# A hybrid decoder trunk on one core: all transposes of its two mixers through the vector engine and DRAM, and 64-row products in alternate halves of the array

## The chip, the cores and the metric

The kernel runs on one core of a Trainium2 chip. The metric is the device time of one launch in microseconds (us). The kernel before takes 1131.28 us, the median of three runs (1131.26 to 1131.33). Engines are named as in the profile: PE (TensorE, matmul), PEld (its weight load), DVE (VectorE), ACT (ScalarE), POOL (GpSimd) and SP (SyncE, which issues nearly all DMAs here).

## The reference

Two layers over a sequence of 256 tokens of width 1024, in float32:

```python
for i in range(DEPTH):                                   # DEPTH = 2
    x = x + 0.5 * swiglu_ffn(rmsnorm(x, ffn1_norm[i]), ffn1_wi[i], ffn1_wo[i])     # width 2816
    z = rmsnorm(x, mix_norm[i]) @ w_in[i]
    mq, mk, mv, mo, mi, mf, sq, sk, sv, ga, gb = jnp.split(z, offsets, axis=-1)
    hA = mlstm_chunkwise(mq, mk, mv, mi + b_igate[i], mf + b_fgate[i])   # 4 heads, qk 64, v 128
    yA = (jax.nn.sigmoid(mo) * rmsnorm(hA, ml_out_norm[i])) @ w_a[i]
    hB = swa_sink_attention(sq, sk, sv, q_norm[i], k_norm[i], sinks[i], rel_bias)
    yB = hB @ w_b[i]                                     # 8 query heads on 2 key heads of 64
    x = x + (jax.nn.sigmoid(ga) * yA + jax.nn.sigmoid(gb) * yB) @ w_out[i]
    x = x + 0.5 * swiglu_ffn(rmsnorm(x, ffn2_norm[i]), ffn2_wi[i], ffn2_wo[i])
    gate = jax.nn.sigmoid(rmsnorm(x, ple_norm[i]) @ w_ple_gate[i])
    x = x + gate * (p[i] @ w_ple[i])
```

`mlstm_chunkwise` is a causal product of q and k, weighted by exp of sums of gates with a running maximum (the gates' sums F, c and M below), times v, divided by a bounded row sum. `swa_sink_attention` normalises q and k per head, adds a position bias, takes the softmax over a window of 128 with a sink per head, and multiplies by v.

## The kernel before, in words

The 256 tokens stand as two tiles t of 128 rows. Every large product takes activations with the contracted width on the partitions: the left operand of a matmul (the one that PE loads as weights) is the transposed activation, the right one the weight matrix from DRAM. For float32 accuracy each operand is split into a high and a low part, and a product is three matmuls (`mm_unit`, L222 to L224: high by low, low by high, high by high).

Weight matrices come in units of up to 1 MB. SP starts their load into one of three `raw` buffers (L190, tile names raw_*), ACT writes the high part (L194, hi_*) and DVE subtracts for the low part (L195, lo_*), each in two halves of 1024 columns, into a ring of four buffers; loads run three units ahead. PE's order is written by hand: the program runs as a stream of units, and after each tile's 12 matmuls of a unit a `tick()` advances every spawned task, a Python generator, to its next `yield`. The constants W_* are numbers of such ticks that a task lets pass before its matmuls or transposes, so that other engines can finish what they need. DVE, ACT, POOL and SP get their orders from a scheduler that follows PE's program.

The FFN's gated hidden tiles h aren't transposed on PE but by `turn_split`: DVE transposes 32x32 blocks (L254, tile inq), SP writes the result to DRAM (L260, scr) and reads it back with the blocks in their places (L265, back), and ACT and DVE split it into high and low (L273, L274).

In the mixer of a layer, PE transposes against an identity. The projections come in the order sq, if (with keys and values of the window attention), mqk, mv, mo, ga0, ga1, gb0, gb1 (tiles z_mix_*). Spawned beside them:
- `swa`, for the queries and keys of the window attention: qk is normalised to qkn (L563, L569) and PE transposes it after W_NORM ticks (tps L579, tpk L582) to qTs and kTs.
- `ep_mqk`: q and k of the mLSTM, transposed on PE (tpq L530), copied to qT and kT (L533, L534).
- `swa_part`: logits (lg, L606), softmax, transposes of its weights L (pt L634) to PT after W_PT ticks, product with v (ov L648) after W_OV, result hb, transposed (tp_hb, L245) after W_HB.
- `ml_gates`: the gates' sums on 4 rows, in the order emt, c, M, lf, F, c, M, emt (L691 to L702); after W_CP ticks PE turns c and emt into columns (cp, L708 and L709), and M goes over DRAM to all rows (Mb).
- `ml_mix` and `ml_out`: st = k by q (L734, L740) times the weights E, then num (L761 and on) and its row sums dd (L767, L768), normalisation, output gate, result ha, transposed after W_HA ticks (tp_ha, L245).

The heads of lg and st have a width of 64, so that each of these matmuls contracts over one half of the array's 128 rows. In `merged`, ya (from w_a) and yb (from w_b) are gated, summed and transposed on PE (tp_mx). The second FFN follows, and beside it the embedding p is transposed on PE (tp_p). Lines of the changed functions that the diff doesn't touch keep their meaning after it.

Of the kernel before, what the change touches and what calls it, by code (L numbers as in the profile page):

```python
# [52 lines left out]
W_NORM = 5  # L53
# [3 lines left out]
W_OV = 2  # L57
# [3 lines left out]
W_HA = 5  # L61
# [3 lines left out]
def trunk_kernel(ctx: ExitStack, tc: tile.TileContext, a: dict, out: bass.AP):  # L65
# [182 lines left out]
    def turn_split(pool, src, nblk, hi, lo, name):  # L248


        n = nblk * P
# [2 lines left out]
        nc.vector.transpose(  # L254
            inq[:, 0:n].rearrange("p (b k s) -> p b k s", b=4, k=nblk),
            src[:, 0:n].rearrange("p (k c b) -> p b k c", c=32, b=4),
        )
# [15 lines left out]
        nc.scalar.copy(hv, bv)  # L273
        nc.vector.tensor_tensor(lv, bv, hv.bitcast(F32), op=ALU.subtract)  # L274

# [194 lines left out]
    def mix_in(pool, i, xn, finish):  # L470
# [21 lines left out]
        qk = pair([P, 10, HD], "qk")  # L492
# [29 lines left out]
        def ep_mqk(t, o, rstd):  # L522
            z = work.tile([P, 512], F32, tag="sg", name=f"mqk{i}_{t}")
            nc.scalar.activation(z, o, AF.Copy, scale=rstd)

            def turn():
                yield
                tp = bank(f"tpq{i}_{t}")
                for b in range(4):
                    nc.tensor.transpose(tp[:, b * P : (b + 1) * P], z[:, b * P : (b + 1) * P], ident)  # L530
                tv = tp.rearrange("p (b s) -> p b s", s=P)
                tok = slice(t * P, (t + 1) * P)
                nc.vector.tensor_copy(qT[:, :, tok], tv[:, 0:2, :])  # L533
                nc.vector.tensor_scalar(kT[:, :, tok], tv[:, 2:4, :], HD**-0.5, None, ALU.mult)  # L534

            spawn(turn())
# [12 lines left out]
        def swa(t):  # L549
# [27 lines left out]
            tp = bank(f"tps{i}_{t}")  # L577
            for j in range(4):
                nc.tensor.transpose(tp[:, j * P : (j + 1) * P], z[:, j * P : (j + 1) * P], ident)  # L579
            nc.scalar.activation(qTs[t], heads(tp, P), AF.Copy, scale=qs)  # L580
            tk = bank(f"tpk{i}_{t}")
            nc.tensor.transpose(tk[:, 0:P], z[:, 4 * P :], ident)  # L582
            nc.scalar.activation(kTs[:, t * P : (t + 1) * P], tk[:, 0:P], AF.Copy, scale=qg[:, 1:2])
            for h0 in range(0, SWQ, 4 * (2 - t)):
                spawn(swa_part(t, h0))

        def swa_part(t, h0):
# [10 lines left out]
            yield  # L598
            L = pool.tile([P, nh, nk], F32, tag="s4", name=f"L{nmp}", bufs=4)
            mx = stat("mx")  # L600
            for j0 in range(0, nh, per):
                g = (h0 + j0) // 4
                rows = slice(HD * g, HD * (g + 1))
                o = heads(bank(f"lg{nmp}_{j0}"), nk)
                for j in range(per):
                    nc.tensor.matmul(  # L606
                        o[:, j, :], qTs[t][rows, (h0 + j0 + j) % 4, :], kTs[rows, 0:nk], start=True, stop=True
                    )
                js = slice(j0, j0 + per)
                nc.vector.tensor_tensor(L[:, js, :], o, bias[:, h0 + j0 : h0 + j0 + per, boff:], op=ALU.add)  # L610
                nc.vector.reduce_max(mx[:, js], L[:, js, :], axis=AX.X)
# [17 lines left out]
            PT = pool.tile([P, t + 1, nh, P], F32, tag="s4", name=f"PT{nmp}", bufs=4)  # L629
            for kt in range(t + 1):  # L630
                for j0 in range(0, nh, 4):
                    tp = bank(f"pt{nmp}_{kt}_{j0}")
                    for j in range(4):
                        nc.tensor.transpose(  # L634
                            tp[:, j * P : (j + 1) * P], L[:, j0 + j, kt * P : (kt + 1) * P], ident
                        )
                    dst = PT[:, kt, j0 : j0 + 4, :]
                    if kt + j0 == 0:
                        nc.scalar.copy(dst, heads(tp, P))
                    else:  # L640
                        nc.vector.tensor_copy(dst, heads(tp, P))
# [3 lines left out]
            for j in range(nh):  # L645
                g = (h0 + j) // 4
                for kt in range(t + 1):
                    nc.tensor.matmul(  # L648
                        ov[:, j * HD : (j + 1) * HD],
                        PT[:, kt, j, :],  # L650
# [11 lines left out]
            hi, lo = abT[t][1]  # L662
            transpose_split(hb, nh * HD // P, hi[:, ks, :], lo[:, ks, :], f"hb{nmp}")
# [53 lines left out]
        def ml_mix():  # L717
# [12 lines left out]
            for par in range(2):  # L730
                rows = slice(HD * par, HD * (par + 1))
                o = bank(f"st0{i}_{par}").rearrange("p (h t s) -> p h t s", t=2, s=P)
                for hh in range(2):
                    nc.tensor.matmul(o[:, hh], kT[rows, hh, 0:P], qT[rows, hh, :], start=True, stop=True)  # L734
# [4 lines left out]
                for hh in range(2):
                    nc.tensor.matmul(o[:, hh], kT[rows, hh, P:S], qT[rows, hh, P:S], start=True, stop=True)  # L740
                for hh in range(2):
                    ev = E2[:, 2 * hh + par, :]
                    nc.vector.tensor_tensor(ev, ev, o[:, hh], op=ALU.mult)
            for t in range(NT):
                yield
                spawn(ml_out(t, E01, E2))

        def ml_out(t, E01, E2):
# [39 lines left out]
            hi, lo = abT[t][0]  # L788
            transpose_split(haf, 4, hi, lo, f"ha{i}_{t}")
# [34 lines left out]
        for n in range(2):  # L824
            oa = [bank(f"ya{i}_{t}_{n}") for t in range(NT)]
            stream(oa, abTs, [f"wa{i}_{n}_0"], 4)
            ob = [bank(f"yb{i}_{t}_{n}") for t in range(NT)]
            stream(ob, abTs, [f"wb{i}_{n}_0"], 4, kbase=4)
# [42 lines left out]
    for i in range(DEPTH):  # L871
# [6 lines left out]
        with tc.tile_pool(name=f"ple{i}", bufs=1, side="right", reuse_waits="tile") as pool:  # L878
            pT = [halves(pool, 2, f"pT{i}_{t}") for t in range(NT)]

            def embed(_):
# [92 lines left out]
```

## Time and profile before

| what | value |
|---|---|
| median of three runs | 1131.28 us (1131.26 to 1131.33) |
| the profiled execution's own time | 1131.24 us |
| its span | 1129.5 us |
| PE busy, share of the span | 1121.0 us, 99% |
| DVE busy | 722.6 us, 64% |
| ACT busy | 585.3 us, 52% |
| POOL busy | 32.7 us, 3% |
| DMA queue of the hardware | 229.99 MB, 61.5% of 16 engines' span |

The span goes from the first to the last instruction of one execution; the time of an execution is a little longer. Busy PE means that a matmul is in flight there. In a group's row the third number behind the bar is the mean duration of one instruction, for a matmul from its start to its end through the pipeline, so that many of them overlap; the pieces of the chain of waits (start, length, engine, tile, line, count) show their pace. An fp32 matmul that isn't split has two passes in the trace.

### The profile page before, as it was taken

What the parts mean: (1) busy time and instruction counts of PE and PEld (TensorE: products, weight loads), DVE (VectorE), ACT (ScalarE), POOL (GpSimd) and SP (SyncE); (2) the same over time, 40 slices, a digit from 0 to 9 for tenths busy, and PEclk for the clock granted to TensorE, in tenths of its full rate; (3) what the DMA queues carried; (4) which work ended last, traced back from release to release, by engine and by line L of the source; (5) the groups of instructions that cost most, each with busy time, mean ns of one, the idle gap of its engine ahead of it and who ended that gap; (6) DMA issues with size and microseconds to landing.
All of it is one profiled execution on the core that took longest, in us unless ns stands there. A gap on an engine that the chain in (4) does not pass through costs nothing.

```text
span 1129.5 us, 13574 instructions
## 1 busy us (share of the span) xinstructions
PE 1121.0 (99%) x5252; PEld 931.7 (82%) x5252; DVE 722.6 (64%) x916; ACT 585.3 (52%) x848; POOL 32.7 (3%) x30
## 2 busy tenths in 40 slices
PE   8999999999999999999999999999999999999998
PEld 7788888888888888888888888888888888888887
DVE  6775745685677566654776666467856766667454
ACT  6444534677645544543664544347865354444352
POOL 1000000100000000000000000001000000000000
PEclk9999999999999999999999999999999999999999
DMA  7897764744464767765557767555545556776641
GB/s 266 277 302 244 237 228 123 231 161 128 171 196 151 258 224 251 248 220 193 179 165 252 257 228 244 189 158 190 169 143 168 185 184 228 254 245 216 228 147 38
DMA packets 130785, 230.86 MB, mean 204 GB/s; under 512 B 12968, under 2 KB 46880, under 8 KB 130720
## 3 DMA queue, kind: packets, MB, share of 16 engines
q1 hardware_dynamic: 130720, 229.99, 61.5%
q8 instruction: 41, 0.67, 0.2%
q14 instruction: 24, 0.20, 0.1%
HBM read 217.37 MB, written 12.60 MB: 204 GB/s over the span
## 4 chain that ended last, share of the span: by engine, by line
PE 97%; DVE 1%; DMA 1%; issue 0%; ACT 0%; SPq 0%
PE h_f L222 14%; PE h_f L223 14%; PE h_f L224 14%; PE acc_f_o L222 7%; PE acc_f_o L224 7%; PE acc_f_o L223 7%; PE z_mix_ga L222 1%; PE z_mix_ga L224 1%; PE z_mix_ga L223 1%; PE z_mix_gb L222 1%; PE acc_wout L222 1%; PE acc_wout L224 1%; PE z_mix_gb L224 1%; PE acc_wout L223 1%; PE z_mix_gb L223 1%; PE acc_pg L224 1%
## 5 line engine op out<-in xcount | busy, mean ns | idle before, releaser
L195 DVE TENSOR_TENSOR lo_f<-raw_f,hi_f 128x1024 fp32r<-128x1024 f32 (+1 forms) x176 | 207.7, 1216 | 100.6 <-ACT hi_f L194 100.2
L194 ACT CAST hi_f<-raw_f 128x1024 fp32r<-128x1024 f32 (+1 forms) x178 | 176.5, 1039 | 163.1 <-PE h_f L224 90.3
L195 DVE TENSOR_TENSOR lo_f_o<-raw_f_o,hi_f_o 128x1024 fp32r<-128x1024 f32 x88 | 103.7, 1220 | 90.0 <-ACT hi_f_o L194 90.0
L194 ACT CAST hi_f_o<-raw_f_o 128x1024 fp32r<-128x1024 f32 x88 | 88.1, 1050 | 113.7 <-PE acc_f_o L224 70.0
L222 PE MATMUL h_f<-lo_f,xT_f_0h 128*128 128x512 f32 x352 | 138.2, 393 | 0.2 <-DVE lo_f L195 0.2
L223 PE MATMUL h_f<-hi_f,xT_f_0l 128*128 128x512 f32 x352 | 137.1, 390 | 1.2 <-DVE xT_f_0l L239 1.2
L222 PE MATMUL h_f<-lo_f,xT_f_1h 128*128 128x512 f32 x352 | 137.2, 390 | 0.5 <-DVE lo_f L195 0.4
L224 PE MATMUL h_f<-hi_f,xT_f_0h 128*128 128x512 f32 x352 | 137.1, 389 | 0.0
L223 PE MATMUL h_f<-hi_f,xT_f_1l 128*128 128x512 f32 x352 | 137.0, 389 | 0.0
L224 PE MATMUL h_f<-hi_f,xT_f_1h 128*128 128x512 f32 x352 | 136.9, 389 | 0.0
L222 PEld LDWEIGHTS h_f<-lo_f,xT_f_0h 128*128 128x128 f32 x352 | 66.1, 188 | 15.0 <-issue 0.6
L222 PEld LDWEIGHTS h_f<-lo_f,xT_f_1h 128*128 128x128 f32 x352 | 66.0, 188 | 15.0 <-DVE lo_f L195 1.4
L223 PEld LDWEIGHTS h_f<-hi_f,xT_f_0l 128*128 128x128 f32 x352 | 66.2, 188 | 14.8 <-DVE xT_f_0l L239 1.6
L224 PEld LDWEIGHTS h_f<-hi_f,xT_f_1h 128*128 128x128 f32 x352 | 66.1, 188 | 13.9
L224 PEld LDWEIGHTS h_f<-hi_f,xT_f_0h 128*128 128x128 f32 x352 | 66.0, 188 | 13.9
L223 PEld LDWEIGHTS h_f<-hi_f,xT_f_1l 128*128 128x128 f32 x352 | 66.0, 188 | 13.6
L222 PE MATMUL acc_f_o<-lo_f_o,hT_f_1h 128*128 128x512 f32 x176 | 68.8, 391 | 0.0
L222 PE MATMUL acc_f_o<-lo_f_o,hT_f_0h 128*128 128x512 f32 x176 | 68.7, 390 | 0.0
L224 PE MATMUL acc_f_o<-hi_f_o,hT_f_1h 128*128 128x512 f32 x176 | 68.5, 389 | 0.0
L224 PE MATMUL acc_f_o<-hi_f_o,hT_f_0h 128*128 128x512 f32 x176 | 68.5, 389 | 0.0
L223 PE MATMUL acc_f_o<-hi_f_o,hT_f_0l 128*128 128x512 f32 x176 | 68.5, 389 | 0.0
L223 PE MATMUL acc_f_o<-hi_f_o,hT_f_1l 128*128 128x512 f32 x176 | 68.5, 389 | 0.0
(359 smaller groups left out, 2045.7 us busy)
## 6 DMA issues: line engine op xcount, KB each, us to landing
raw_f<-in_ffn_wi_dram SPq DMA_DIRECT2D x79, 1024.0 KB, 5.2
raw_f_o<-in_ffn_wo_dram SPq DMA_DIRECT2D x44, 1024.0 KB, 5.0
scr_h_f<-inq_h_f SPq DMA_DIRECT2D x40, 256.0 KB, 3.9
back_h_f<-scr_h_f SPq DMA_DIRECT2D x40, 256.0 KB, 4.7
raw_f<-in_ffn_wi_dram SPq DMA_DIRECT2D x18, 512.0 KB, 4.4
raw_z_ga<-in_w_in_dram SPq DMA_DIRECT2D x8, 1024.0 KB, 5.4
raw_z_gb<-in_w_in_dram SPq DMA_DIRECT2D x8, 1024.0 KB, 5.3
raw_wout<-in_w_out_dram SPq DMA_DIRECT2D x8, 1024.0 KB, 4.9
```

Source lines behind the costliest of these rows:

```text
L194: nc.scalar.copy(hi[:, o:e], raw[:, o:e])
L195: (nc.gpsimd if between and o // step % 2 == 0 else nc.vector).tensor_tensor(lo[:, o:e], raw[:, o:e], hi[:, o:e].bitcast(F32), op=ALU.subtract
L222: nc.tensor.matmul(o, xh, wl[:, k, sl], start=start, stop=False)
L223: nc.tensor.matmul(o, xl, wh[:, k, sl], start=False, stop=False)
L224: nc.tensor.matmul(o, xh, wh[:, k, sl], start=False, stop=stop)
```

## The change

All transposes inside the mixers and that of the embedding take the way that h has. `turn` is `turn_split` without the split, and can write the turned tile in the order "s k" (token outside, block inside), so that the 4 or 5 blocks of one token lie side by side: qkTs is [128, 256 tokens, 5] (4 query blocks and one of keys), qkT [128, 256, 4], and PT has its four heads innermost. The matmuls of lg, st and ov then read columns with a step of 4 or 5 floats. Gains are put on qkTs in place by ACT; k of the mLSTM is scaled in `ep_mqk`. lg and st use two banks, one for each half of the rows, and alternate between the halves. W_NORM goes from 5 to 2, W_OV from 2 to 1, W_HA from 5 to 3; a turn has ticks of its own, one more than before. w_b is loaded and multiplied before w_a. The inq tiles of the mixers and of the embedding share two buffers (tag "xg") with work tiles, ha shares with qk, and lf is kept in ln. Transposes of x, of the merged mx and of the gates cp remain on PE.

```diff
-W_NORM = 5
+W_NORM = 2
 W_CP = 6
 W_MB = 2
 W_PT = 3
-W_OV = 2
+W_OV = 1
 W_HB = 1
-W_HA = 5
+W_HA = 3
...
-            specs.extend(by_cols(a["w_a"][i], 512, cols, f"wa{i}_{n}"))
             specs.extend(by_cols(a["w_b"][i], 512, cols, f"wb{i}_{n}"))
+            specs.extend(by_cols(a["w_a"][i], 512, cols, f"wa{i}_{n}"))
...
+    def turn(inq, src, dst, name, order="k s"):
+        k = src.shape[1]
+        w = k * 32
+        n = 4 * w
         nc.vector.transpose(
-            inq[:, 0:n].rearrange("p (b k s) -> p b k s", b=4, k=nblk),
-            src[:, 0:n].rearrange("p (k c b) -> p b k c", c=32, b=4),
+            inq[:, 0:n].rearrange(f"p (b {order}) -> p b k s", b=4, k=k),
+            src.rearrange("p k (c b) -> p b k c", b=4),
         )
         yield
...
+        nc.sync.dma_start(dst, bass.AP(tensor=s0.tensor, offset=s0.offset, ap=[[w, P], [32 * n, 4], [1, w]]))
+        yield
+        yield
...
-        qT = pool.tile([P, 2, S], F32, name=f"qT{i}")
-        kT = pool.tile([P, 2, S], F32, name=f"kT{i}")
+        qkT = pool.tile([P, S, 4], F32, name=f"qkT{i}")
-        qTs = pair([P, 4, P], "qTs")
-        kTs = pool.tile([P, S], F32, name=f"kTs{i}")
+        qkTs = pool.tile([P, S, 5], F32, name=f"qkTs{i}")
...
+            yield from turn_qk(qkTs, z, t, f"qk{i}_{t}")
+            tok = slice(t * P, (t + 1) * P)
+            for part, gain in ((qkTs[:, tok, 0:4], qs), (qkTs[:, tok, 4], qg[:, 1:2])):
+                nc.scalar.activation(part, part, AF.Copy, scale=gain)
+            spawn(swa_logits(t))
...
+            for k0 in range(0, 4, per):
+                os = [heads(bank(f"lg{i}_{t}_{k0}_{g}"), nk) for g in range(SWKV)]
+                for j in range(per):
+                    for g in range(SWKV):
+                        rows = slice(HD * g, HD * (g + 1))
+                        nc.tensor.matmul(
+                            os[g][:, j, :],
+                            qkTs[rows, t * P : (t + 1) * P, k0 + j],
+                            qkTs[rows, 0:nk, 4],
...
-                        PT[:, kt, j, :],
+                        PT[:, kt, j // 4, :, j % 4],
...
-            transpose_split(hb, nh * HD // P, hi[:, ks, :], lo[:, ks, :], f"hb{nmp}")
+            yield from turn_split(pool, inq_tile(f"hb{nmp}"), blocks(hb), hi, lo, f"hb{nmp}")
...
+            for hh in range(2):
+                for o, rows in zip(os, half):
+                    nc.tensor.matmul(
+                        o[:, hh].rearrange("p t s -> p (t s)"),
+                        qkT[rows, 0:P, 2 + hh],
+                        qkT[rows, :, hh],
...
-            transpose_split(haf, 4, hi, lo, f"ha{i}_{t}")
+            yield from turn_split(pool, inq_tile(f"ha{i}_{t}"), blocks(haf), *abT[t][0], f"ha{i}_{t}")
...
-                    transpose_split(pin[t], 2, pT[t][0], pT[t][1], f"p{i}_{t}")
+                    inq = work.tile([P, 5 * P], F32, tag="xg", name=f"inq_p{i}_{t}")
+                    yield from turn_split(pool, inq, blocks(pin[t]), *pT[t], f"p{i}_{t}")
```

Three places of the order, each before and then after. The first is DVE's order in layer 0, from the last steps of qkn's normalisation to the end of the gates' sums (s, v: its sums of squares; emt, c, M, F: the gates; lo_z_mo and lo_z_ga: low parts of weight units of the output gate and of the first merge gate). Its beginning before:

```order
L555 TENSOR_REDUCE s_0_1_1780<-sqk_1_1778 128x10
L195 TENSOR_TENSOR lo_z_mo_1811<-raw_z_mo_1809,hi_z_mo_1810 128x1024
L557 TENSOR_SCALAR v_0_1_1782<-s_0_1_1780 128x10
L195 TENSOR_TENSOR lo_z_mo_1811<-raw_z_mo_1809,hi_z_mo_1810 128x1024
L563 TENSOR_TENSOR qkn_1_1786<-qk_1_1548,r_0_1_1784 128x4x64 x2
L569 TENSOR_TENSOR qkn_1_1786<-qk_1_1548,r_0_1_1784 128x128
L691 TENSOR_SCALAR emt_1572<-ln_1567 4x256
L693 SCALAR_TENSOR_TENSOR c_1570<-emt_1572,ln_1567 4x256
```

The same place after:

```order
L569 TENSOR_REDUCE s_0_1_1774<-sqk_1_1772 128x10
L255 STREAM_TRANSPOSE inq_qk_0_1823<-qkn_0_1756 128x4x5x32
L571 TENSOR_SCALAR v_0_1_1776<-s_0_1_1774 128x10
L195 TENSOR_TENSOR lo_z_mo_1805<-raw_z_mo_1803,hi_z_mo_1804 128x1024
L577 TENSOR_TENSOR qkn_1_1780<-qk_1_1548,r_0_1_1778 128x4x64 x2
L583 TENSOR_TENSOR qkn_1_1780<-qk_1_1548,r_0_1_1778 128x128
L195 TENSOR_TENSOR lo_z_mo_1805<-raw_z_mo_1803,hi_z_mo_1804 128x1024
L721 TENSOR_SCALAR emt_1566<-ln_1562 4x256
L255 STREAM_TRANSPOSE inq_qk_1_1839<-qkn_1_1780 128x4x5x32
L723 SCALAR_TENSOR_TENSOR c_1564<-emt_1566,ln_1562 4x256
```

Two transposes have come in, and the second half of lo_z_mo stands behind qkn_1 instead of ahead of it. The end of the sums on DVE, before:

```order
L698 SCALAR_TENSOR_TENSOR F_1569<-ones,lf_1568 4x256
L699 TENSOR_TENSOR c_1570<-gp_1790,F_1569 4x256
L700 SCALAR_TENSOR_TENSOR M_1571<-ones,c_1570 4x256
L701 TENSOR_TENSOR emt_1572<-F_1569,M_1571 4x256
L195 TENSOR_TENSOR lo_z_ga_0_1904<-raw_z_ga_0_1902,hi_z_ga_0_1903 128x1024
```

And after:

```order
L728 SCALAR_TENSOR_TENSOR F_1563<-ones,ln_1562 4x256
L255 STREAM_TRANSPOSE inq_mqk_0_1888<-mqk_0_1841 128x4x4x32
L729 TENSOR_TENSOR c_1564<-gp_1784,F_1563 4x256
L255 STREAM_TRANSPOSE inq_mqk_1_1890<-mqk_1_1846 128x4x4x32
L730 SCALAR_TENSOR_TENSOR M_1565<-ones,c_1564 4x256
L195 TENSOR_TENSOR lo_z_ga_0_1894<-raw_z_ga_0_1892,hi_z_ga_0_1893 128x1024
L731 TENSOR_TENSOR emt_1566<-F_1563,M_1565 4x256
```

Two more transposes and half a unit of z_ga now stand ahead of emt's last addition (L701 before, L731 after).

The second is SP's order in layer 0, where the loads of the merge gate gb and of w_a and w_b are issued. Before:

```order
L190 DMA raw_z_gb_4_2307<-in_w_in_dram 128x4x512
L190 DMA raw_z_gb_0_2371<-in_w_in_dram 128x4x512
L190 DMA raw_z_gb_4_2443<-in_w_in_dram 128x4x512
L190 DMA raw_wa_0_0_2475<-in_w_a_dram 128x4x512
L190 DMA raw_wb_0_0_2527<-in_w_b_dram 128x4x512
```

After (inq_PT and scr_PT are the turned softmax weights on their way to and from DRAM):

```order
L190 DMA raw_z_gb_0_2309<-in_w_in_dram 128x4x512
L261 DMA scr_PT_1_4_0_0_2197<-inq_PT_1_4_0_0_2169 128x512
L261 DMA scr_PT_1_4_1_0_2199<-inq_PT_1_4_1_0_2170 128x512
L265 DMA PT_1_0_2163<-scr_PT_1_0_0_0_2193 128x4x128
L265 DMA PT_1_0_2163<-scr_PT_1_0_1_0_2195 128x4x128
L190 DMA raw_z_gb_4_2417<-in_w_in_dram 128x4x512
L190 DMA raw_wb_0_0_2469<-in_w_b_dram 128x4x512
L190 DMA raw_wa_0_0_2513<-in_w_a_dram 128x4x512
L265 DMA PT_1_4_2168<-scr_PT_1_4_0_0_2197 128x4x128
L265 DMA PT_1_4_2168<-scr_PT_1_4_1_0_2199 128x4x128
```

The writes and reads of PT stand between the weight loads, and the reads of PT_1_4, the last of them, behind raw_wb_0_0 and raw_wa_0_0.

The third is PE's order at the logits of tile 0 in layer 0 (lg; the digits behind it are layer, tile and first head). Before:

```order
L606 MATMUL lg_0_0_0_1952<-kTs_1561,qTs_0_1559 128x128 x4
L606 MATMUL lg_0_0_4_1959<-kTs_1561,qTs_0_1559 128x128 x4
```

After (the last digit is now the half of the rows):

```order
L616 MATMUL lg_0_0_0_1983<-qkTs_1558 128x128
L616 MATMUL lg_0_0_1_1984<-qkTs_1558 128x128
L616 MATMUL lg_0_0_0_1983<-qkTs_1558 128x128
L616 MATMUL lg_0_0_1_1984<-qkTs_1558 128x128
L616 MATMUL lg_0_0_0_1983<-qkTs_1558 128x128
L616 MATMUL lg_0_0_1_1984<-qkTs_1558 128x128
L616 MATMUL lg_0_0_0_1983<-qkTs_1558 128x128
L616 MATMUL lg_0_0_1_1984<-qkTs_1558 128x128
```

Four matmuls of one half and then four of the other have become pairs.

More of the change, by code (lines that the diff above doesn't have):

```diff
@@ L490, in pair, with over_qk @@
             return [pool.tile(shape, F32, name=f"{name}{i}_{t}") for t in range(NT)]
-        qk = pair([P, 10, HD], "qk")
+        def over_qk(shape, name):
+            return [pool.tile(shape, F32, tag=f"qk{t}", name=f"{name}{i}_{t}") for t in range(NT)]
+        qk = over_qk([P, 10, HD], "qk")
         vsw = pair([P, P], "vsw")
@@ L523, in ep_mqk, with turned @@
             z = work.tile([P, 512], F32, tag="sg", name=f"mqk{i}_{t}")
-            nc.scalar.activation(z, o, AF.Copy, scale=rstd)
-            def turn():
-                yield
[L528 to L536, printed above, removed]
+            nc.scalar.activation(z[:, 0 : 2 * P], o[:, 0 : 2 * P], AF.Copy, scale=rstd)
+            rk = small.tile([P, 1], F32, tag="rk", name=f"rk{i}_{t}")
+            nc.vector.tensor_scalar(rk, rstd, HD**-0.5, None, ALU.mult)
+            nc.scalar.activation(z[:, 2 * P :], o[:, 2 * P :], AF.Copy, scale=rk)
+            def turned():
+                yield
+                yield from turn_qk(qkT, z, t, f"mqk{i}_{t}")
+            spawn(turned())
         def ep_mv(t, o, rstd):
@@ L576, in swa, with swa_logits @@
                 yield
[L577 to L587, printed above, removed]
+            yield from turn_qk(qkTs, z, t, f"qk{i}_{t}")
[3 more added lines that the diff above has]
+            spawn(swa_logits(t))
+        def swa_logits(t):
+            yield
             nk = P * (t + 1)
@@ L591, in swa_part @@
             nh = SWQ if t == 0 else SWQ // SWKV
+            parts = []
+            for h0 in range(0, SWQ, nh):
+                nmp = f"{i}_{t}_{h0}"
+                L = pool.tile([P, nh, nk], F32, tag="s4", name=f"L{nmp}", bufs=4)
+                mx = small.tile([P, nh], F32, tag=f"mx{t}{h0}", name=f"mx{nmp}", bufs=1)
+                parts.append((h0, L, mx))
+            for k0 in range(0, 4, per):
[7 more added lines that the diff above has]
+                            qkTs[rows, 0:nk, 4],
+                            start=True,
+                            stop=True,
+                        )
+                for g in range(SWKV):
+                    head = 4 * g + k0
+                    h0, L, mx = parts[head // nh]
+                    js = slice(head - h0, head - h0 + per)
+                    nc.vector.tensor_tensor(L[:, js, :], os[g], bias[:, head : head + per, boff:], op=ALU.add)
+                    nc.vector.reduce_max(mx[:, js], L[:, js, :], axis=AX.X)
+            for h0, L, mx in parts:
+                gen = swa_part(t, h0, nh, L, mx)
+                spawn(gen)
+                advance(gen)
+        def swa_part(t, h0, nh, L, mx):
             part = slice(h0, h0 + nh)
@@ L596, in stat @@
                 return small.tile([P, nh], F32, tag=f"{name}{t}{h0}", name=f"{name}{nmp}", bufs=1)
[L598 to L611, printed above, removed]
             m = stat("m")
@@ L628, in swa_part @@
                 yield
[L629 to L641, printed above, removed]
+            PT = pool.tile([P, t + 1, nh // 4, P, 4], F32, tag="s4", name=f"PT{nmp}", bufs=4)
+            turns = [
+                turn(
+                    inq_tile(f"PT{nmp}_{kt}_{q}"),
+                    L[:, 4 * q : 4 * q + 4, kt * P : (kt + 1) * P],
+                    PT[:, kt, q].rearrange("p (a s) j -> p a (s j)", a=4),
+                    f"PT{nmp}_{kt}_{q}",
+                    "s k",
+                )
+                for kt in range(t + 1)
+                for q in range(nh // 4)
+            ]
+            for _ in zip(*turns):
+                yield
             for _ in range(W_OV):
@@ L673, in mix_in @@
         s0 = scr[:, :]
-        ln, lf, F, c, M, emt = (row(n) for n in ("ln", "lf", "F", "c", "M", "emt"))
+        ln, F, c, M, emt = (row(n) for n in ("ln", "F", "c", "M", "emt"))
         def ml_gates():
@@ L824, in mix_in @@
         for n in range(2):
+            ob = [bank(f"yb{i}_{t}_{n}") for t in range(NT)]
+            stream(ob, abTs, [f"wb{i}_{n}_0"], 4, kbase=4)
             oa = [bank(f"ya{i}_{t}_{n}") for t in range(NT)]
             stream(oa, abTs, [f"wa{i}_{n}_0"], 4)
[L827 to L828 removed]
             for t in range(NT):
```

73 lines of the change are left out of this document (42 added, 31 removed).

## The prediction

> **What bounds the kernel now.** I read the head of the page first, then the share of each engine in the chain that ended last, then that chain's pieces inside the mixer.
>
> ```profile
> span 1129.5 us, 13574 instructions
> PE 1121.0 (99%) x5252; PEld 931.7 (82%) x5252; DVE 722.6 (64%) x916; ACT 585.3 (52%) x848; POOL 32.7 (3%) x30
> PE 97%; DVE 1%; DMA 1%; issue 0%; ACT 0%; SPq 0%
> ```
>
> PE is busy for 99% of the span and is 97% of the chain. So PE work taken out is time gained, at full price, and a wait put into PE's row is time lost, at full price. DVE at 64% looks free, but that is a mean: what counts is what stands ahead of a needed result in DVE's own order. The profiled execution took 1131.24 us, its span and 1.74 us around it; the median of the runs is 1131.28, so sums against 1131.24 stand for the median to 0.04 us.
>
> **1. Transposes leave PE.** These are the groups that go, with their counts for both layers:
>
> ```profile
> L634 PE MATMUL pt<-ident,L 128*128 128x128 f32 x48 | 5.9, 272 | 0.0
> L245 PE MATMUL tp_ha<-ident,ha 128*128 128x128 f32 x16 | 2.4, 272 | 0.0
> L579 PE MATMUL tps<-ident,qkn 128*128 128x128 f32 x16 | 2.4, 272 | 0.0
> L245 PE MATMUL tp_hb<-ident,hb 128*128 128x128 f32 x16 | 2.4, 271 | 0.0
> L530 PE MATMUL tpq<-ident,mqk 128*128 128x128 f32 x16 | 2.1, 272 | 0.0
> L245 PE MATMUL tp_p<-ident,pin 128*128 128x128 f32 x8 | 1.2, 272 | 0.0
> L582 PE MATMUL tpk<-ident,qkn 128*128 128x128 f32 x4 | 1.1, 272 | 0.0
> ```
>
> 48+16+16+16+16+8+4 = 124. The 272 ns is the latency of one; what PE gives up per transpose is its pace, which the chain has:
>
> ```profile
> 253.71 1.75 PE pt L634 x16
> 235.63 0.23 PE z_mix_mv L224
> 236.88 1.64 PE lg L606 x16
> 241.46 2.90 PE lg L606 x16
> 258.22 1.73 PE ov L648 x16
> 280.84 0.89 PE num L761 x8
> ```
>
> 1.75/16 = 0.109 us, so 124 x 0.109 = **-13.5 us**. What replaces them runs on DVE, SP's queue and ACT; where that is late is items 3 and 5. For ha and hb it isn't: after the last ov eight gb units of 12 matmuls (12 x 0.23 = 2.8 us, one tick) stand before w_b, 22 us, and w_a comes after w_b now; a turn is two transposes, out and back, by the rows below 2.2 + 3.9 + 4.7. I cost them at nothing; without that cover it would be those 10.8 us. The embedding's turn lies beside the second FFN, as h's do now: nothing.
>
> **2. Halves in turn.** Logits and st use 64 rows of the array each. Before, they pair only where one half's row ends and the other's begins:
>
> ```profile
> 269.91:272.38 2.47, 2.47 (x17) 2.15 (x16) 1.44 (x5) 1.12 (x3) 0.00 (x0) 1.00 0.46 78
> 270.87 0.27 PE L740 MATMUL st<-qT,kT 64*128 64x128 f32 x1
> 270.88 0.48 PE L734 MATMUL st<-qT,kT 64*128 64x256 f32 x1
> 271.20 0.38 PE L734 MATMUL st<-qT,kT 64*128 64x256 f32 x1
> 271.21 0.27 PE L740 MATMUL st<-qT,kT 64*128 64x128 f32 x1
> 271.42 0.59 PE L734 MATMUL st<-qT,kT 64*128 64x256 f32 x2
> ```
>
> Matmuls of the two halves start 10 ns apart (270.87 and 270.88, 271.20 and 271.21): they run side by side. In one half, 256 columns start every 0.22 us (271.20 to 271.42) and 128 every 0.11. The trace has two passes for each of these matmuls. With every pass paired: the 16 passes of tile 0's logits take 8 x 0.11 = 0.9 plus a tail, 1.0 where 1.64 stood; tile 1's 8 x 0.22 = 1.8, 1.9 for 2.90; st's 4 x 0.22 + 4 x 0.11 = 1.3, 1.5 for 2.47. That is 2.6 a layer, **-5.2 us**; not all pairs may meet, so 0 to -5.2.
>
> **3. A new wait at cp.** PE turns c and emt (L708, L709) W_CP ticks after the gates; W_CP is unchanged. This is what DVE does ahead of it:
>
> ```profile
> 221.20 1.22 DVE L195 TENSOR_TENSOR lo_z_mo<-raw_z_mo,hi_z_mo 128x1024 fp32r<-128x1024 f32 x1
> 222.34 0.17 DVE L557 TENSOR_SCALAR v<-s 128x10 f32<-128x10 f32 x1
> 225.48 0.76 DVE L563 TENSOR_TENSOR qkn<-qk,r 128x256 f32<-128x256 f32 x2 [1.85 <-POOL r L287]
> 233.75 0.41 DVE L701 TENSOR_TENSOR emt<-F,M 4x256 f32<-4x256 f32 x1
> 234.20 0.42 ACT L702 ACTIVATE emt<-emt 4x256 f32<-4x256 f32 x1 [2.41 <-DVE emt L701]
> 236.47 0.22 PE L708 MATMUL cp<-ident,c 4*128 4x4 f32 x1
> L254 DVE STREAM_TRANSPOSE inq_h_f<-hh_f 128x512 f32<-128x512 f32 x40 | 44.1, 1102 | 1.3
> L254 DVE STREAM_TRANSPOSE inq_h_f<-hh_f 128x256 f32<-128x256 f32 x8 | 5.1, 633 | 0.3
> L274 DVE TENSOR_TENSOR hT_f_1l<-back_h_f,hT_f_1h 128x512 fp32r<-128x512 f32 x20 | 13.8, 692 | 27.3 <-ACT hT_f_1h L273 27.1
> L274 DVE TENSOR_TENSOR hT_f_1l<-back_h_f,hT_f_1h 128x256 fp32r<-128x256 f32 x4 | 1.7, 426 | 4.5 <-ACT hT_f_1h L273 4.5
> ```
>
> emt is ready at 234.20 + 0.42 = 234.62, used at 236.47: 1.85 us of slack. In the new order five things are put ahead of emt's last addition. A transpose of 640 columns costs 1102 + 128 x (1102 - 633)/256 ns = 1.34 us. (a) qk_0's transpose takes the place of one lo half: 1.34 - 1.22 = +0.12. (b) That lo half, before done under the 1.85 us that DVE waited for POOL, now stands behind qkn_1: +1.22. (c) qk_1's transpose: +1.34. (d) Two mqk transposes of 512: +2.20. (e) One lo half of z_ga: +1.22. Starts follow 0.08 us before the end of the one ahead (221.20 + 1.22 against 222.34), five times: -0.4. Sum 5.7, emt at 240.3. PE meanwhile comes earlier: 8 tpq, 8 tps and 2 tpk of the layer stood ahead of cp, so 236.47 - 18 x 0.109 = 234.5. PE then waits 240.3 - 234.5 = 5.8 us, in both layers, as the order is the same in both: **+11.6 us**. Queued behind the wait are the logits and every z unit; nothing else feeds PE. Bounds: the DVE idles a little in this stretch and may catch up 1.3 us a layer (9); writes of the token order "s k" may cost the transposes up to 1.7 (15). ACT's new part, two gain scalings behind qk_0's round trip, ends by about 237 (transposed by 225, out and back 3.9 + 4.7 by the rows of item 5, four short operations) and is under the same wait.
>
> **4. The clock after that wait.** The trace shows a slow pace at the start and the granted clock falling at the end:
>
> ```profile
> 1.05 4.63 PE L850 MATMUL warm<-ones 128*128 128x128 f32 x20 [1.05 <-DVE half_neg L89]
> 1124.63 0.28 PE L224 MATMUL acc_pg<-hi_pg,xT_ple_1h 128*128 128x256 f32 x1
> 1127.00:1129.50 2.50, 0.00 (x0) 0.00 (x0) 0.00 (x0) 0.00 (x0) 0.00 (x0) 0.81 0.17 56
> ```
>
> 20 passes in 4.63 us are 0.23 each where 0.109 is the pace later: half speed for about 4.4 us. After the last matmul (1124.63 + 0.28) the clock means 0.81 over 1127.0 to 1129.5, which is 1.0 for 1.55 us and 0.5 for 0.95: it falls about 3.65 us into the idle. A wait of 5.8 us is longer, so PE would come back at half speed, for 0 to 4.4 us, which loses 0 to 2.2; near the start's row, less the part that passes before the fall is over, 1.5 a layer, **+3.0 us**. The Trainium skill, TensorE: Matmul & The Clock Gate, Part 1, says that about 3.4 us of idle halve the clock and that about 3.4 us of work restore it; by that the term would be 2 x 1.7 = +3.4, an estimate from that page, and the end of this trace agrees with it (3.65).
>
> **5. The last turn of the weights PT.** SP's order puts PT_1_4's reads back behind raw_wa_0_0, whose buffer comes free by a lo half behind dd on DVE:
>
> ```profile
> 283.10 0.23 DVE L767 TENSOR_TENSOR dd<-dd,cem 128x2 f32<-128x2 f32 x2
> 283.24 1.22 DVE L195 TENSOR_TENSOR lo_z_gb<-raw_z_gb,hi_z_gb 128x1024 fp32r<-128x1024 f32 x1
> scr_h_f<-inq_h_f SPq DMA_DIRECT2D x40, 256.0 KB, 3.9
> back_h_f<-scr_h_f SPq DMA_DIRECT2D x40, 256.0 KB, 4.7
> raw_wa<-in_w_a_dram SPq DMA_DIRECT2D x4, 1024.0 KB, 5.2
> ```
>
> num of tile 0 ends at 280.84 + 0.89 = 281.7, that lo half at 284.46, 2.7 later. The reads then land 4.7 us later if they go beside the 1 MB, or 5.2 + 4.7 if behind it: 7.4 to 12.6 us after num. PE has a unit (2.8), ov of tile 0 (1.73), num of tile 1 (2 x 0.89), a unit (2.8) and half an ov (0.87) up to PT_1_4's: 10.0. So 0 to 2.6 a layer; I take 1.0, a little under the middle, as both are spread over the same 16 engines at once: **+2.0 us** (0 to 5.2).
>
> **6. Reads with a stride.** lg, st and ov now read qkTs, qkT and PT with a step of 16 or 20 bytes between columns; no PE read in this trace has one. Of other engines the rows of item 3 do: L254 reads with a step of 16 bytes, 469 ns for 256 more columns, 1.83 ns each; L274, side by side, 266 ns, 1.04 each. The ratio is 1.76. On PE it ranges from 1 to 2.1 (1.83 ns against PE's 0.109 us/128 = 0.85). I take 1.76 as the only strided read that is measured: 0.76 x (0.9 + 1.76 + 1.3) = 3.0 for lg and st, and ov's 48 passes a layer at 1.73/16 = 0.108 give 0.76 x 5.2 = 4.0. 7.0 a layer, **+14.0 us** (0 to +20), of which ov's first part covers the +2.0 of item 5. The Trainium skill, Advanced Engine Details and Errata, Memory Cachelines, has a penalty where each access falls into another 16-byte line; it gives no figure for PE, speaks against this change, and by it the full-rate case below falls.
>
> **Sum.** 1131.24 - 13.5 - 5.2 + 11.6 + 3.0 + 14.0 = **1141.1 us**.
>
> **Rivals.** *Full rate*: strided reads cost PE nothing, as a weight load may be hidden. For it: PE's columns have their own pace, and no row shows PE slowed by an address. Against it: the factor on DVE. 1141.1 - 14.0 + 2.0 = 1129.1 (1123.5 to 1134), the other side. *No wait at cp*: DVE catches up, as it is 64% busy and its idle stands mostly before ACT's casts; from 5.8 us of catching up on, PE doesn't stop. Against it: between 226 and 234 DVE's gates are one dependent chain. 1141.1 - 11.6 - 3.0 = 1126.5 with slow reads, also faster; 1114.5 with neither. *SP's queue*: full rate, but turns that stand ahead of raw_z_gb and raw_wb wait for their writes to land (3.9), and PE starves at gb for 2 to 3 us a layer: 1129.1 + 5 = 1134. *Pairs don't overlap* only takes item 2 away: +5.2, inside the ranges.
>
> **How the numbers follow.** Slow reads with the wait 0.52, own range 1134 to 1148; full rate 0.25; no wait 0.10; SP's queue 0.13. A measurement tells 0.2% here, 2.3 us: 1129.0 to 1133.5 is no change. Faster: half of full rate (0.13), no wait (0.10), a tail (0.02). Same: the rest of full rate (0.12), a part of SP's queue (0.05). Slower: 0.58. The range goes from 1124, the lower end of full rate, to 1147, near the upper end of slow reads; outside it lie the last of those tails and "neither", under 0.1.
>
> **What would show it.** Item 1: the seven groups gone, DVE transposes of 128x512 and 128x640 in their place. 2: lg and st starting in pairs some 10 ns apart. 3: PE idle ahead of cp, released by ACT's emt, 5 to 7 us in each layer. 4: a granted clock under 1 just behind. 5: PE idle before ov of PT_1_4, released by a DMA. 6: starts of lg farther apart than 0.11 or 0.22 us, ov's x16 near 3.0 instead of 1.73. The forecast is wrong if ov keeps 0.108 a pass, or if cp doesn't wait.

## The result, and the profile after

The changed kernel takes 1151.79 us (median of four runs, 1150.06 to 1152.31) against 1131.3: a ratio of 1.0175, 95% interval 1.016 to 1.019. It is slower by 20.5 us where 10 were forecast, and outside the range. The profiled execution took 1150.06 us. The head of the page and its chain:

```profile
span 1148.3 us, 13468 instructions
PE 1129.8 (98%) x5128; PEld 936.1 (82%) x5128; DVE 745.0 (65%) x940; ACT 585.5 (51%) x846; POOL 31.1 (3%) x30
PE 93%; DVE 4%; issue 1%; ACT 1%; POOL 1%; DMA 0%; SPq 0%
```

PE has 124 instructions fewer (5252 to 5128) and is busy for 8.8 us longer: the work that is left has become slower. It also waits, as the list of PE's waits says (waits in total, times, longest):

```profile
PE cp L739 <- ACT emt L732: 6.3, 2, 3.2
PE cp L738 <- DVE c L729: 3.6, 2, 1.8
```

That is 9.9 us for both layers, on c and then on emt. The slowed work is seen in the pieces of the chain of layer 0:

```profile
247.36 2.16 PE lg L616 x16
252.46 3.99 PE lg L616 x16
267.57 2.13 PE st L764 x8
269.70 0.93 PE st L778 x8
282.68 3.55 PE ov L678 x16
290.82 7.33 PE ov L678 x32
```

Before, these were 1.64, 2.90, 2.47 in all for st, 1.73 and 3.5. The clock isn't the reason: it is at 1.00 from 245 to 290 us. The last thing is in no row of PE's work but in the granted clock (last but two in each row of the table by stretches; the columns ahead of it are busy times):

```profile
235.00:240.00 5.00, 0.49 (x4) 0.43 (x4) 5.00 (x7) 1.53 (x3) 0.00 (x0) 0.65 0.87 252
240.00:245.00 5.00, 5.00 (x17) 4.00 (x17) 2.78 (x4) 3.16 (x5) 0.00 (x0) 0.66 1.02 317
290.00:295.00 5.00, 5.00 (x24) 4.92 (x22) 3.31 (x12) 3.31 (x8) 1.07 (x2) 0.96 0.19 54
295.00:300.00 5.00, 5.00 (x19) 4.62 (x19) 2.81 (x6) 1.53 (x3) 0.00 (x0) 0.50 0.00 0
300.00:305.00 5.00, 5.00 (x20) 4.03 (x20) 2.53 (x4) 0.00 (x0) 0.00 (x0) 0.86 0.53 161
```

It falls in the wait at cp (0.65), as forecast. It falls a second time, to 0.50, while PE is busy with ov (290.82 to 298.15) and stays there for some 3 us of the gb units behind.

From the start times of PE's matmuls in both profiles, added by tile over both layers, after less before (a tile's stretch here and below is the sum of the times from the start of each of its matmuls to the start of the next one on PE):

| stretch | us |
|---|---|
| transposes gone (pt, tp_ha, tp_hb, tp_p, tps, tpk, tpq) | -12.6 |
| ov, 10.4 to 21.6 | +11.2 |
| lg, 9.1 to 12.3, and st, 5.0 to 6.1 | +4.4 |
| waits around cp (gap in front of it, in mv's stretch, and inside it) | +10.1 |
| z_mix_mo behind cp, at half clock | +3.6 |
| z_mix_gb behind ov, at half clock | +3.3 |
| z_mix_ga | -0.6 |

The sum is +19.4; the spans differ by 18.8.

### The profile page after: what moved, and what is told of

Its sections match the earlier page's. It is cut to its first block, busy times and chain, and to the rows that moved or that the text cites. A ratio compares the mean times of both kernels' runs of the same rounds, so it can differ in the third digit from the quotient of the medians.

```text
span 1148.3 us, 13468 instructions
## 1 busy us (share of the span) xinstructions
PE 1129.8 (98%) x5128; PEld 936.1 (82%) x5128; DVE 745.0 (65%) x940; ACT 585.5 (51%) x846; POOL 31.1 (3%) x30
## 4 chain that ended last, share of the span: by engine, by line
PE 93%; DVE 4%; issue 1%; ACT 1%; POOL 1%; DMA 0%; SPq 0%
PE h_f L222 14%; PE h_f L223 14%; PE h_f L224 14%; PE acc_f_o L222 7%; PE acc_f_o L223 7%; PE acc_f_o L224 7%; PE ov L678 2%; PE z_mix_gb L222 1%; PE z_mix_gb L223 1%; PE z_mix_gb L224 1%; PE z_mix_ga L222 1%; PE acc_wout L224 1%; PE acc_wout L222 1%; PE z_mix_ga L224 1%; PE acc_wout L223 1%; PE z_mix_ga L223 1%
## 5 line engine op out<-in xcount | busy, mean ns | idle before, releaser
L222 PEld LDWEIGHTS h_f<-lo_f,xT_f_1h 128*128 128x128 f32 x352 | 66.1, 188 | 15.1 <-DVE lo_f L195 1.4
```

The lines of the kernel that those rows point to most:

```text
L222: nc.tensor.matmul(o, xh, wl[:, k, sl], start=start, stop=False)
```

## The experiments

**What the step costs, and whether the wait at cp is DVE's order.** Four kernels, all from the changed one. a_cp8 moves cp two ticks on:

```diff
-W_CP = 6
+W_CP = 8
```

> The changed kernel with W_CP 8 instead of 6: cp stands two ticks (2 x 2.77 us) later in PE's order. Theory (PE waits 4.95 us a layer for DVE's sums, and the clock falls in that wait): the wait and the 1.7 us a layer at half clock behind it go, 1151.8 - 9.9 - 3.4 = 1138.5 us. Rival (the sums are late for what comes after cp as well: Mb, the weights E, st): the wait only moves to st or num, 1149 to 1152 us.

1136.54 us (1135.32 to 1138.74), 1.0045 of the kernel before (95% interval in brackets, here and below) [1.0029, 1.0060], 15.3 us less than the changed kernel. No wait at cp is left in its list, and z_mix_mo is back at 22.7 us from 26.4. The wait and the half clock behind it were real, and nothing else needed those sums earlier.

a_pt reads PT back with tokens side by side; a block of 32 tokens is then a packet of its own, so that each turn takes four DMAs:

```diff
-            PT = pool.tile([P, t + 1, nh // 4, P, 4], F32, tag="s4", name=f"PT{nmp}", bufs=4)
+            PT = pool.tile([P, t + 1, nh // 4, 4, P], F32, tag="s4", name=f"PT{nmp}", bufs=4)
...
-                        PT[:, kt, j // 4, :, j % 4],
+                        PT[:, kt, j // 4, j % 4, :],
```

> The changed kernel, but PT is read back with the blocks outside and the tokens side by side (four DMAs of 64 KB a turn instead of one of 256 KB), so that ov's weights are contiguous again; lg and st keep their step. Theory (a step of 16 bytes doubles PE's weight load, and the clock falls while PE waits inside such loads): ov's passes go from 0.22 back to 0.108 us, -11.2 us, and the clock stays at 1.0 behind ov, -3.3: 1137 us. Rival (ov is slow for another reason, its 64 columns or the DMAs beside it): ov stays at 0.22 a pass, 1150 to 1153 us. If the smaller packets are late, PE waits ahead of ov for a DMA.

1137.13 us (1135.98 to 1138.22), 1.0048 [1.0033, 1.0063]. Its chain, and the stretch behind ov:

```profile
284.39 1.73 PE ov L684 x16
290.72 3.52 PE ov L684 x32
```

```profile
290.00:300.00 10.00, 10.00 (x62) 8.88 (x61) 8.45 (x21) 4.90 (x13) 1.01 (x1) 1.00 0.72 204
```

ov is at 0.108 to 0.110 us a pass again, the clock stays at 1.00. Undoing this one layout takes back 14.7 us of the 20.5.

a_all does the same for qkTs and qkT:

> The changed kernel with PT, qkTs and qkT all read back with tokens side by side, so that no PE read has a step; halves still alternate. Theory: beside a_pt's gain lg and st lose the factor 2 and pair fully: lg and st from 9.2 us a layer to 4.4, another -9.6: 1127.5 us. Rival (pairing brings nothing of its own, lg and st come back to before's 7.0 a layer): -4.4, 1132.5 us.

1137.77 us (1136.28 to 1139.41), 1.0054 [1.0037, 1.0071]: no better than a_pt, 10 us over the expectation. But lg and st did what was expected:

```profile
247.55 1.09 PE lg L623 x16
251.59 1.93 PE lg L623 x16
264.66 1.06 PE st L770 x8
265.73 0.44 PE st L784 x8
```

1.09 and 1.93 where 2.16 and 3.99 stood, 1.50 where 3.06 did. Contiguous halves do run side by side, and the step had cost a factor of 2.0 in all of them. What PE gained it gave back some 30 us later: it came to ov of tile 1 before PT was back, and ov's stretch is 17.3 us over both layers instead of 10.4, with gb at half clock again (47.1 instead of 43.8).

a_all_cp8 has both edits:

> Both edits, contiguous reads and W_CP 8. If they add: 1127.5 - 13.3 = 1114 us, faster than the kernel before by 1.5%. If DVE is late for something else behind cp, 1127 us.

1132.83 us (1130.44 to 1135.01), 1.001 [0.9999, 1.002]. PE's list of waits says where most of the 18.8 us between this and the expectation went:

```profile
PE ov L684 <- DMA PT<-scr_PT: 6.5, 3, 5.8
PE ov L684 <- DVE dd L819: 5.1, 1, 5.1
```

The long wait of each row is the one ahead of the products with PT_1_4, 5.8 us in layer 0 and 5.1 in layer 1; the list blames DVE for the second, but there too a read of PT landed at 842.51, 0.14 us before PE went on. With these waits and the slow passes behind them ov's stretch is 26.3 us, 15.9 over its own 10.4; gb at half clock makes another 3.3. With PE faster, PT's way round is the limit. In SP's order the eight reads of PT_1_4 stand right behind two loads of gb and one of w_b, much as item 5 of the prediction had it; in layer 1 the first of them lands 9.6 us after SP began to issue it.

**Whether ov can wait for PT.** W_OV 4 in place of 1, on a_all_cp8:

> The changed kernel with contiguous reads, W_CP 8 and W_OV 4 instead of 1: the products with PT stand three ticks (8.3 us) later. Theory (in a_all_cp8 all that was gained ahead of ov came back as a wait of PE for PT's round trip, 8.2 and 7.6 us, and as half clock behind it): wait and half clock go, 1132.8 - 15.8 - 3.3 = 1114 us. Rival (PT's round trip is bound by the queue and moves along, or hb is then late for w_b): 1122 to 1132 us with a new wait ahead of ov or yb.

1135.64 us (1134.08 to 1136.79), 1.0039 [1.0026, 1.0052]: the rival's wait, and 3.6 us above the rival's range. ov's stretch is 10.4, but now hb is late for w_b; this is PE's longest wait, and a part of SP's queue (start, length of the group, instructions):

```profile
PE yb L222 <- ACT abT_1h L283: 14.5, 2, 7.7
```

```profile
269.80 4.77 SPq L267 DMA_DIRECT2D PT<-scr_PT  x7
276.31 11.25 SPq L267 DMA_DIRECT2D PT<-scr_PT  x8
300.00 0.33 SPq L261 DMA_DIRECT2D scr_hb<-inq_hb  x1
313.12 0.36 SPq L272 DMA_DIRECT2D back_hb<-scr_hb  x1
```

SP issues in order, and the issue of the eight reads of PT_1_4 takes it 11.25 us, where a write of hb takes 0.33; its list of waits has only 0.8 us on a semaphore for reads of PT. The eight are not alike: 0.80, 3.08, 2.25, 1.30 and 1.98 us, and then three of 0.51, which is also the median of all reads of PT here. They stand right behind three loads of 1 MB. In a_pt, where the same eight are issued some 7 us behind the last of these loads, seven of them take 0.37 to 0.51 and one 1.49. By themselves, then, four reads for one cost 1.5 us more of issue a turn (four of 0.51 for one, which has the same median in the changed kernel). The packets of 128 bytes don't make the issue longer than that; that the loads still on their way do is argued from the order and wasn't tried by itself.

Nor is it what makes hb late here. The eight are issued by 287.6, and the first write of hb goes out at 300.00, as soon as DVE has turned hb. PE ended ov of tile 1 at 291.0; DVE makes its two parts of hb only at 299.9 and 300.8, and the last read of hb is issued at 313.12, behind a wait for DVE to have used up an earlier one, and lands at 317.6. What is late is hb's own way round, which starts three ticks later.

**Which step costs.** a_pt2 turns PT two blocks at a time, with one DMA each, so that ov's weights have a step of 8 bytes:

```diff
-            PT = pool.tile([P, t + 1, nh // 4, P, 4], F32, tag="s4", name=f"PT{nmp}", bufs=4)
+            PT = pool.tile([P, t + 1, nh // 2, P, 2], F32, tag="s4", name=f"PT{nmp}", bufs=4)
...
-                    L[:, 4 * q : 4 * q + 4, kt * P : (kt + 1) * P],
+                    L[:, 2 * q : 2 * q + 2, kt * P : (kt + 1) * P],
...
-                for q in range(nh // 4)
+                for q in range(nh // 2)
```

> The changed kernel, but PT is turned two blocks at a time, so that ov's weights have a step of 2 floats (8 bytes) instead of 4 (16 bytes); DVE issues 12 transposes of 256 columns a layer for 6 of 512. Theory A (the price comes with one used value per 16-byte line, as the Trainium skill, Advanced Engine Details and Errata, Memory Cachelines has it): two values a line, ov at 0.108 us a pass, 1137 us, as a_pt. Theory B (any step costs the factor 2): ov stays at 0.22 and the clock falls behind it, 1152 us. Between: 0.16 a pass, 1145 us.

1136.48 us (1136.41 to 1137.91), 1.0049 [1.0034, 1.0064], as a_pt. Two values of every 16 bytes are nearly enough, 0.114 and 0.116 us a pass where a_pt has 0.108 and 0.110:

```profile
283.10 1.82 PE ov L678 x16
289.50 3.71 PE ov L678 x32
```

b_steps measures it alone. Behind the end of the kernel before stand probes like these, on columns of x with a step of w or m floats; its outputs are those of the kernel before:

```diff
+    def probe(w, m, name, count=32):
+        o = bank(name)[:, 0 : m.shape[1]]
+        for _ in range(count):
+            nc.tensor.matmul(o, w, m, start=True, stop=True)
```

> The kernel before, and behind its last product a row of probes on PE that its outputs don't use: 32 fp32 matmuls (64 passes) each, with a step of 1, 2, 3, 4, 5 or 8 floats between the columns of the weights (w) or of the moving operand (m), 32 contiguous ones ahead of each. Theory (a step past two values a 16-byte line costs a factor 2, on either operand): 0.109 us a pass at steps 1 and 2, about 0.22 at 4, 5 and 8, the same for w and m; 3 in between; w and m at 4 together 0.22 if the reads are behind each other's cover, 0.33 if they add; clock under 1 in or behind the slow probes. Rival (only weights pay): m stays at 0.109. Some 14 x (7 + 7 to 14) us, 1131 + 250 to 300 us in all.

1397.55 us in one run. Nine of the fifteen groups of its last 270 us (name with the steps of weights and moving operand; busy time is what counts, over 64 passes):

```profile
L925 PE MATMUL base<-ones 128*128 128x128 f32 x871 | 99.7, 275 | 0.0
L925 PE MATMUL w8m1n<-x 128*128 128x128 f32 x64 | 15.4, 401 | 0.0
L925 PE MATMUL w4m4n<-x 128*128 128x128 f32 x64 | 15.3, 417 | 0.0
L925 PE MATMUL w4m1n<-x 128*128 128x128 f32 x64 | 15.1, 397 | 0.0
L925 PE MATMUL w4m1n<-x 128*128 128x64 f32 x64 | 15.1, 423 | 0.0
L925 PE MATMUL w1m4n<-x 128*128 128x128 f32 x64 | 14.7, 405 | 0.0
L925 PE MATMUL w3m1n<-x 128*128 128x128 f32 x64 | 11.3, 337 | 0.0
L925 PE MATMUL w2m1n<-x 128*128 128x128 f32 x64 | 7.7, 281 | 0.0
L925 PE MATMUL w1m2n<-x 128*128 128x128 f32 x64 | 7.4, 274 | 0.0
```

A pass is 0.114 us at step 1 (99.7/871), 0.120 and 0.116 at 2, 0.177 at 3, 0.236 and 0.230 at 4, 0.241 at 8; of the groups not shown, step 5 is at 0.222 (weights) and 0.233 (moving), and the moving operand alone at 0.175 (step 3) and 0.236 (step 8). Weights and moving operand pay alike, and both at 4 pay once (0.239): the two reads don't add up. 0.236 us over 128 columns is 1.84 ns a column. The row at 3 suggests what is paid for: 128 columns at 12 bytes lie in 96 pieces of 16 bytes, and 96 x 1.84 ns is 0.177 us. So an estimate from these rows is the larger of 0.89 ns a column (0.114/128) and 1.84 ns for each 16 bytes that the columns touch.

**Why the clock fell in ov.** b_ov2 is the kernel before with each matmul of ov issued twice, which makes a contiguous run as long as the strided one:

```diff
-            for j in range(nh):
+            for j in [j for j in range(nh) for _ in range(2)]:
                 g = (h0 + j) // 4
```

> The kernel before with every matmul of ov issued twice (the second overwrites the first): its longest run becomes 64 passes at 0.108 us, 7.0 us, as long as the changed kernel's strided run of 32. Theory A (the clock falls behind ov because PE waits for strided weights in it): clock stays 1.0, +10.4 us for the passes alone, 1141.7 us. Theory B (it falls in any 7 us of ov, as 64 columns behind 128 of weights leave the array idle): clock at 0.5 behind it, 1144 to 1145 us.

1141.92 us (1141.65 to 1142.23), 1.0095 [1.0078, 1.0111]: the passes alone, and no fall:

```profile
264.84 7.09 PE ov L648 x64
```

```profile
260.00:280.00 20.00, 20.00 (x137) 17.98 (x137) 7.96 (x17) 10.82 (x18) 0.00 (x0) 1.00 0.34 106
```

Yet a step of 4 is not enough for it: the probes of b_steps with 128 moving columns kept 1.00, and those with 64, at the same pace, did not (stretches of the two):

```profile
1179.30:1194.20 14.90, 14.90 (x66) 14.90 (x65) 0.00 (x0) 0.00 (x0) 0.00 (x0) 1.00 0.00 0
1379.80:1394.90 15.10, 15.08 (x66) 14.89 (x64) 0.00 (x0) 0.00 (x0) 0.00 (x0) 0.67 0.00 0
```

At 0.114/128 = 0.89 ns a column, 64 columns keep the array multiplying for 57 ns of 236, 24% of the time; 128 columns for 48%; contiguous 64 columns for 50%. The clock fell at 24% and stayed at 48%. So the strided ov, 64 columns behind 128 slow weights, seems to count as idle though PE's row shows it busy. The time fits: the 0.96 of the stretch from 290 to 295 puts the fall some 3.8 us behind ov's start at 290.82, and at the end of the kernel before it came 3.65 us into the idle; in the probe it took about 5 us (0.67 over 15.1). That the share of multiplying decides is argued from these three cases; where between 24 and 48% it turns is open.

**Halves in turn, alone.** b_alt puts only the alternation into the kernel before:

> The kernel before with the logits and st alternating between the halves of the rows, all else (transposes on PE, contiguous reads, W_*) as it was. Theory (halves run side by side where operands are contiguous): lg from 9.1 to 6.0 us and st from 5.0 to 3.0 over both layers, 1131.3 - 5.0 = 1126.3 us. Rival (PE's gain there is lost in later work, which waits for DVE's additions to the logits): 1129 to 1131.5 us.

1128.35 us (1128.07 to 1130.7), 0.9977 [0.9967, 0.9986]. lg and st took 6.0 and 3.0 us over both layers, as expected, but only 2.8 of the 5.0 us arrived. Its chain goes through ACT's exponentials into the transposes of the softmax weights:

```profile
252.81 1.98 ACT L L639 x8
254.83 0.77 PE pt L652 x5
```

PE is there earlier than before, ACT isn't: pt's stretch grew from 4.9 to 7.0.

**A version without the costs.** c_best1 keeps all turns on DVE and DRAM, but with no step over 2 on PE and no more DMAs than one a turn: PT as in a_pt2, q and k of the mLSTM in pairs too, and the gains of the window attention written by ACT from the turned tile into contiguous ones; W_CP 8.

```diff
-                nc.scalar.activation(part, part, AF.Copy, scale=gain)
+            nc.scalar.activation(qTs[t], zT[:, :, 0:4].rearrange("p s k -> p k s"), AF.Copy, scale=qs)
+            nc.scalar.activation(kTs[:, tok], zT[:, :, 4], AF.Copy, scale=qg[:, 1:2])
```

> The changed kernel with no step over 2 floats on PE and one DMA for each turned tile: PT and the mLSTM's q and k turned two blocks at a time, qk's gains written by ACT from the turned tile into contiguous ones; W_CP 8. If SP's many short DMAs (48 for PT) were what made PT late in a_all_cp8: 1151.8 - 13.3 - 14.5 - 9.4 = 1114.6 us. If the round trip itself is too long for the time that PE now leaves it: a wait of up to 8 us a layer ahead of ov and half clock behind it, 1122 to 1132 us.

1128.27 us (1126.89 to 1129.28), 0.9972 [0.9962, 0.9982]; PE still waits for PT, in the list and in ov's stretch of 17.8. But now it is tile 0's PT that is late (3.3 and 3.8 us in the two layers), and num and ga behind it lose time at a lower clock (0.54 from 278 to 282 us). PT_1_4, which held PE in a_all_cp8, comes in time. The list's row:

```profile
PE ov L692 <- DMA PT<-scr_PT: 7.1, 4, 2.9
```

> The same with W_OV 2, ov one tick (2.77 us) later. If c_best1 still waits ahead of ov, up to 5.5 us less of it, over both layers; if hb is then late for w_b, as in a_all_cp8_ov4, no gain or a loss of up to 5 us.

1123.05 us (1120.95 to 1127.78), 0.9939 [0.9916, 0.9961], the fastest here: ov's stretch is 14.4, and the wait that the list puts down to PT is

```profile
PE ov L692 <- DMA PT<-scr_PT: 0.8, 2, 0.4
```

beside 1.7 us ahead of tile 1's ov that it puts down to DVE. z_mix_gb's stretch is 48.7 where 43.7 is full pace; it holds these 1.7, and the other 3.3, 1.6 us a layer, are lost behind ov at a lower clock:

```profile
284.00:290.00 6.00, 6.00 (x33) 5.52 (x33) 4.58 (x13) 4.17 (x8) 1.92 (x2) 0.72 1.05 336
```

> c_best2 with W_OV 3, ov one tick later still. c_best2 waited 2.0 us a layer inside ov of tile 1 for PT's last reads and for DVE, and lost 2.4 us a layer at half clock behind that. Theory (the clock falls because ov's 64-column products with waits between them keep the array mostly idle): without the wait both go, 1123.0 - 8.8 = 1114 us. Rival (hb is now late for w_b): a wait ahead of yb instead, 1120 to 1126 us.

1128.03 us (1124.96 to 1128.9), 0.9962 [0.9948, 0.9976]. ov's stretch is down to 10.9, but yb's is up from 21.8 to 33.9:

```profile
PE yb L222 <- ACT abT_1h L276: 5.2, 5, 2.1
PE yb L223 <- DVE abT_1l L277: 1.8, 3, 1.3
```

PT and hb are two round trips one behind the other between the softmax and w_b. By these three runs PE's work between them isn't enough for both in this order of units; W_OV only says in front of which of them PE waits.

## Why the prediction was wrong, point by point

- **Item 1** (transposes, -13.5): -12.6 measured. Right; a transpose is 0.102 us from start to start over pt's 48. Its cover for ha, hb and the embedding held: no wait ahead of yb in the changed kernel.
- **Item 2** (halves, -5.2): right. In a_all lg and st come to 4.5 us a layer, where 4.4 were worked out, and the two of a pair start some 7 ns apart. In the changed kernel the step took more than all of it back (9.2, where the kernel before has 7.0).
- **Item 3** (wait at cp, +11.6): 9.9. The five things ahead of emt are there as read from the order, among them qk's second transpose and an lo half behind qkn; emt was ready at 239.66 instead of 240.3. PE stopped at c first, 1.8 us, which the prediction didn't have:

```profile
227.83 1.38 DVE L255 STREAM_TRANSPOSE inq_qk<-qkn 128x640 f32<-128x640 f32 x1
234.85 1.06 DVE L255 STREAM_TRANSPOSE inq_mqk<-mqk 128x512 f32<-128x512 f32 x1
236.12 1.08 DVE L255 STREAM_TRANSPOSE inq_mqk<-mqk 128x512 f32<-128x512 f32 x1
239.24 0.42 ACT L732 ACTIVATE emt<-emt 4x256 f32<-4x256 f32 x1 [3.47 <-DVE emt L731]
239.71 0.27 PE L739 MATMUL cp<-ident,emt 4*128 4x4 f32 x1 [3.17 <-ACT emt L732]
```

- **Item 4** (clock behind it, +3.0): +3.6. Right.
- **Item 5** (PT_1_4): no wait in the changed kernel, its cover by slow reads held. In a_all and a_all_cp8, where that cover is gone, PE waits there, and it costs more than the 0 to 2.6 us a layer that I gave (by ov's stretches 4.0 and 2.9 in a_all, 8.2 and 7.6 in a_all_cp8, where PT comes in four reads for one).
- **Item 6** (reads with a step, +14.0): this step failed. The mechanism was right, the size was not. The contiguous kernels give lg and st 4.5 us and ov 5.25 a layer, the changed one 9.2 and 10.9: 10.3 a layer, +20.6. I took DVE's ratio, 1.76, for PE. A ratio carries the other engine's own pace with it. What carried over here is the time for a value: 1.83 ns on DVE, 1.84 on PE by the probes, against PE's 0.89, a factor of 2.07; that both engines pay the same for the same reason is argued from this one pair of numbers. The prediction had that quotient (2.1), as the upper end.
- **Not in the sum**, which put it at nothing: the second fall of the clock, in ov, +3.3. I had looked for idle time in PE's row, and there is none there.

With the sizes measured: 1141.1 + 0.9 (item 1) - 1.7 (3) + 0.6 (4) + 6.6 (6) + 3.3 = 1150.8, beside 1150.06 of the profiled execution. The rival "full rate" is refuted by b_steps, "no wait at cp" by the list of waits, "SP's queue", PE starving at gb, is in no list of PE's waits; what came as soon as PE was faster was the wait for PT of item 5, and then the one for hb. The Trainium skill's Memory Cachelines (Advanced Engine Details and Errata), cited as speaking against the change, is borne out on PE: at least two hits in 16 bytes are needed, and a step of 2 floats runs close to the pace of 1 (0.116 to 0.120 us against 0.114), 4 at half of it (0.236).

## What to carry to other kernels

Before an operand is laid out for the DMA's sake, count how many of its values PE finds in 16 bytes: two floats are nearly free (2 to 5% here), one costs twice the time on either operand, and half-size turns kept the transposes off PE without that cost. Where a price for one engine is taken from another, try the time of a value before the ratio. When work leaves a saturated engine for a longer way round, the next limit is the way's length: look for everything that stands in order behind it, and move its user with it only as far as the next user has room.

## What the runs showed of the hardware that I had not expected

- The granted clock falls while PE's row is 100% busy: 0.50 behind 7.3 us of ov with strided weights, 0.67 in the probes of 64 columns with a step of 4, but 1.00 in 7.1 us of the contiguous ov, in 7.3 us of contiguous probes of 64 columns and in the probes of 128 columns with the same step. The slow passes themselves aren't slowed by it (15.1 us in both probes); what follows is, by 1.6 us a layer here.
- A step on both operands costs no more than on one (0.239 against 0.236 us a pass).
- SP's issue of a DMA isn't a fixed cost: 0.33 us for hb's turned tile, 0.51 for most reads of PT in packets of 128 bytes, but 0.80 to 3.08 for five such reads right behind three loads of 1 MB.
- Runs of the kernels whose clock falls on the way spread by 1.5 to 7 us (1120.95 to 1127.78 in c_best2), most of those of the kernel before by less than 1. In c_best2 the mean granted clock was 0.998 in the fastest run and 0.992 in the slowest, so a part of it is how much work meets the half clock.
